# Forgetting attention with its heads in pairs: score products alternate between the two row halves, value products carry high and low parts in one operand

## The chip, the core and the metric

The kernel runs on one core of a Trainium2 chip. The metric is the device time of one execution in microseconds (us). The core has a matrix engine (TensorE, PE in the profile, with its weight loads as PEld), a vector engine (VectorE, DVE), an activation engine (ScalarE, ACT), a general engine (GpSimd, POOL) and queues that start transfers (SyncE, SP). Products go from PE into eight banks of the accumulation memory (PSUM); DVE and ACT read them out of there.

## What is computed

Two transformer blocks of width 1024 on 512 tokens. The change lies in the first block's attention, in the eight "forgetting" heads: causal softmax attention whose logits get a bias from cumulated forget gates.

```python
def forgetting_attention(q, k, v, log_f):
    b, s, h, d = q.shape          # 1, 512, 8, 64
    c = jnp.cumsum(log_f, axis=1)
    ...
        sc = jnp.einsum('bqhd,bshd->bhqs', qi, k).astype(jnp.float32) * scale
        bias = jnp.transpose(ci, (0, 2, 1))[..., None] - c_keys[:, :, None, :]
        causal = kpos[None, :] <= qpos[:, None]
        sc = jnp.where(causal[None, None], sc + bias, -jnp.inf)
        p = jax.nn.softmax(sc, axis=-1).astype(v.dtype)
        return jnp.einsum('bhqs,bshd->bqhd', p, v)
```

The rest of the first block is a projection of the normalised tokens (w_in), eight sliding-window heads, an output projection with residual, and a squared-relu MLP. The second block has its own attention and MLP. All inputs are 32-bit floats.

## The kernel before

Every 32-bit operand is split into a high and a low part, each of a one-pass format, and a product is three passes: high by high, high by low, low by high (`mm3`, lines 151 to 154). `split` (line 146) writes the high part with ACT (line 147) and the low part with DVE (line 148). Transposes are products with an identity matrix.

`attention_one` is one phase. `project` computes the projection in chunks of 384 columns, token tile by token tile of 128 tokens: chunks 0 and 1 for the sliding-window heads (tiles named `pj`, `ta`, `sa`, `oa`), chunks 2 to 5 for the four pairs of forgetting heads (`project_b`). `gates` makes the operands `bq` and `bk` of the gate bias: DVE copies each head's log gate to 4 of 32 columns (line 548), PE sums them up along the tokens (tile `cps`, line 558).

`attn_b(pair, ...)` handles two heads. The queries of head 0 lie in partitions 0 to 63, those of head 1 in 64 to 127. Its steps are (u, h, tt): half of the tokens u, head h, token tile tt in the half. For query tile t = 2u + tt the step covers n = 128 (t + 1) keys:

- `scores`: five products into one bank of the ring `s` (two banks, 5 and 6): three of 64 rows (queries by keys, high and low), the causal mask as a product of 128 rows (line 679), the gate bias as a product of 128 rows (line 680) with an operand `bqi` that keeps only this head's rows. Then DVE takes the row maximum (line 683), ACT the exponential with its sum (line 685), DVE the reciprocal (line 686), and DVE or, for the last tile of head 1, ACT scales the row (line 194 or 192). A probability tile has the tag `p`, of which there are three.
- `turn`: t + 1 transposes of the probabilities (tile `tb`, line 703), split into `pbh` and `pbl`.
- `values`: for each key tile three products with 64 stationary columns (line 577): V high by P high, V high by P low, V low by P high. They add up in the one bank of the ring `o` (bank 2). After head 1, `mixed` splits both heads' sums from that bank into `mixT`, the operand of the output projection.

The loop keeps `turn` two steps behind `scores` (LA = 2), and `interleave` spreads the next pair's projection between the steps. The order in which the instructions stand on the engines is made when the program is built: a scheduler in the building layer reorders all of them by its own model of time. Each engine then works off its list in order. For the last pair there is no projection left; what stands between its steps are products of the output projection (tiles `o`, named `o10_0` and so on, in the same ring positions as the projection's banks, and `o10_2`, which needs bank 2).

## Time and profile before

| | |
|---|---|
| device time, 3 runs | 1271.56, 1274.99, 1276.72 us; median 1274.99 |
| profiled execution, first to last instruction (its own total is not listed apart) | 1270.8 us |
| PE busy | 1227.1 us (97%) |
| DVE, ACT, POOL busy | 750.8, 539.2, 257.5 us |
| forgetting heads, first score product to first product of `o10_2` | 122.0 to 238.0 us of the span |
| PE idle in that stretch | 0.90 + 0.20 + 1.87 us |

An engine's busy time counts an instruction from its start to its modelled end. Matmuls overlap: the end of one lies behind the start of the next. How long PE is held by one is therefore read as the distance from its start to the start of the next, not from its duration.

### The profile page before, as it was taken

The numbers are of one execution on the slowest core, as the hardware profiler recorded it, in microseconds if no ns is written. First come the engines' busy times: TensorE is split into PE (matmuls) and PEld (weight loads), VectorE is DVE, ScalarE is ACT, GpSimd is POOL, SyncE is SP. The second block draws the span as 40 slices with busy tenths as digits, with TensorE's granted clock in tenths as the row PEclk, the third lists the DMA queues.
The fourth block names the chain that finished last, engine by engine and source line by source line (L and its number), as shares of the span: only waits on it lengthen the run. The fifth ranks groups of instructions, "written<-read, shape, count | busy, mean of one in ns | idle before, by whom it ended". The sixth has DMA issues, their size and how long they took to land. (4 is left out here: it accounts for less than half of the span.)

```text
span 1270.8 us, 16908 instructions
## 1 busy us (share of the span) xinstructions
PE 1227.1 (97%) x6388; PEld 1027.8 (81%) x6388; DVE 750.8 (59%) x1320; ACT 539.2 (42%) x1032; POOL 257.5 (20%) x328
## 2 busy tenths in 40 slices
...
GB/s 163 64 73 68 26 63 67 133 186 148 198 239 257 234 100 116 63 131 122 67 176 129 51 67 74 64 59 178 82 117 83 100 100 67 130 69 67 149 50 84
DMA packets 147290, 140.22 MB, mean 110 GB/s; under 512 B 14025, under 2 KB 115160, under 8 KB 147208
## 3 DMA queue, kind: packets, MB, share of 16 engines
...
q14 instruction: 32, 0.26, 0.1%
...
## 5 line engine op out<-in xcount | busy, mean ns | idle before, releaser
L898 DVE SCALAR_TENSOR_TENSOR macc<-mod,silu_c,macc 128x1024 f32<-128x1024 f32 x56 | 76.7, 1379 | 13.8 <-DMA mod<-in_w_mod_dram 13.7
L1245 POOL TENSOR_SCALAR ss<-ss 128x1 f32<-128x1 f32 x4 | 1.8, 442 | 328.5 <-ACT sk L1243 328.5
L1280 DVE TENSOR_TENSOR y<-m2d,y 128x512 f32<-128x512 f32 x24 | 16.6, 691 | 60.4 <-PE m2d L154 60.3
L975 DVE SCALAR_TENSOR_TENSOR xa<-m1d,r,xa 128x512 f32<-128x512 f32 x32 | 23.8, 745 | 37.2 <-PE m1d L154 37.2
L147 ACT ACTIVATE m2hid<-m2sq 128x512 fp32r<-128x512 f32 x32 | 20.2, 631 | 38.9 <-DVE m2sq L844 38.9
L147 ACT ACTIVATE m1hid<-m1sq 128x512 fp32r<-128x512 f32 x32 | 20.0, 629 | 38.1 <-DVE m1sq L844 38.1
...
L148 DVE TENSOR_TENSOR m2hid<-m2sq,m2hid 128x512 fp32r<-128x512 f32 x32 | 22.1, 691 | 19.0 <-ACT m2hid L147 18.9
L148 DVE TENSOR_TENSOR npl<-t,nph 128x512 fp32r<-128x512 f32 x32 | 21.7, 681 | 16.4 <-ACT nph L147 16.3
L181 POOL TENSOR_SCALAR w<-w,g_attn 128x384 f32<-128x384 f32 x20 | 26.1, 1314 | 11.2 <-DMA w<-in_w_in_dram 6.6
L148 DVE TENSOR_TENSOR m1hid<-m1sq,m1hid 128x512 fp32r<-128x512 f32 x32 | 21.9, 686 | 9.1 <-ACT m1hid L147 9.1
L194 POOL TENSOR_SCALAR p<-p,d 128x512 f32<-128x512 f32 x8 | 14.0, 1752 | 56.6 <-DVE d L1116 26.3
L683 DVE TENSOR_REDUCE mb<-sb 128x1 f32<-128x128 f32 (+3 forms) x32 | 15.6, 486 | 16.7 <-PE sb L680 16.6
L1115 ACT ACTIVATE p<-s,m 128x512 f32<-128x512 f32 x32 | 22.0, 688 | 6.2 <-DVE m L1113 6.2
L685 ACT ACTIVATE pb<-sb,mb 128x128 f32<-128x128 f32 (+3 forms) x32 | 16.8, 525 | 16.4 <-DVE mb L683 16.1
L843 ACT ACTIVATE m1re<-m1up 128x512 f32<-128x512 f32 x32 | 18.6, 582 | 9.0 <-PE m1up L154 8.7
L1069 POOL TENSOR_TENSOR tb<-G,nam 128x256 f32<-128x256 f32 x24 | 17.7, 765 | 22.6 <-DVE m L1109 12.5
L147 ACT ACTIVATE nph<-t 128x512 fp32r<-128x512 f32 x32 | 19.0, 595 | 7.4 <-PE t L1126 7.2
L844 DVE SCALAR_TENSOR_TENSOR m1sq<-m1up,m1re 128x512 f32<-128x512 f32 x32 | 21.8, 681 | 0.1
L844 DVE SCALAR_TENSOR_TENSOR m2sq<-m2up,m2re 128x512 f32<-128x512 f32 x32 | 21.8, 682 | 0.0
L1126 PE MATMUL t<-ident,p 128*128 128x128 f32 x128 | 18.4, 276 | 1.9 <-DVE npl L148 1.9
L147 ACT ACTIVATE pbh<-tb 128x128 fp32r<-128x128 f32 (+3 forms) x32 | 13.8, 434 | 14.9 <-PE tb L703 14.7
...
## 6 DMA issues: line engine op xcount, KB each, us to landing
...
```

The lines of the kernel that those rows point to most:

```text
L147: self.nc.scalar.activation(out=hi, in_=src, func=AF.Copy)
L148: (eng or self.nc.vector).tensor_tensor(out=lo, in0=src, in1=hi.bitcast(F32), op=ALU.subtract)
L181: eng.tensor_scalar(out=rv[:, i], in0=rv[:, i], scalar1=g, scalar2=None, op0=ALU.mult)
L685: ac(out=pr[:, 0:n], in_=s[:, 0:n], func=AF.Exp, bias=m[:, 0:1], accum_out=den[:, 0:1])
L843: ac(out=r, in_=acc, func=AF.Relu)
L844: nc.vector.scalar_tensor_tensor(out=s, in0=acc, scalar=0.0, in1=r, op0=ALU.max, op1=ALU.mult)
L898: nc.vector.scalar_tensor_tensor(out=accs[s], in0=rw, scalar=sc[:, s, k:k + 1], in1=accs[s], op0=ALU.mult, op1=ALU.add)
L975: nc.vector.scalar_tensor_tensor(out=x[t][:, cols], in0=acc, scalar=r2[:, t:t + 1], in1=x[t][:, cols], op0=ALU.mult, op1=ALU.add)
L1069: nc.gpsimd.tensor_tensor(out=tb[:, h, y], in0=G[:, h, ::-1, o:o + 32][:, :, ::-1], in1=nam[:, y, :].unsqueeze(1).to_broadcast([P, 8, 32]) ...
L1115: ac(out=pr, in_=s, func=AF.Exp, bias=m[:, 2:3], accum_out=den[:, 0:1])
L1126: nc.tensor.transpose(out=tps[:, j * P:(j + 1) * P], in_=pr[:, j * P:(j + 1) * P], identity=self.ident)
L1280: nc.vector.tensor_tensor(out=y[t][:, cols], in0=acc, in1=y[t][:, cols], op=ALU.add)
```

## The change

One step now holds both heads of a pair. Into the two banks of the ring `s`, one per head, go first the eight products of 64 rows, head 0 and head 1 in turn, in an order that is tied down instruction by instruction (`issue_after`). The gate bias is among them: `gates` puts the log gates of all heads into columns 64 to 95 as well, so `bqi` (one tile per pair, not two) has head 0's rows in the lower half and head 1's in the upper. The two causal masks of 128 rows come last. Then come the maximum, exponential, reciprocal and scaling of head 0 and of head 1. The transposes are one step behind (LAB = 1).

The values' high and low parts lie side by side in one tile `vb`, head by head, so that one product has 128 stationary columns, (V high | V low), and each key tile takes two products: by P high and by P low. The bank then holds the high sums in partitions 0 to 63 and the low ones in 64 to 127. After head 1, ACT copies the lower sums of both heads (64 partitions by 512) into a tile of the tag `p`, DVE adds the upper ones to it, and `mixed` splits from that tile.

```diff
-    used = r < 32
+    used = r % 64 < 32
...
-    for h in range(8):
-        c[:, C_PSEL + h] = r // 4 == h
+    for pair in range(4):
+        c[:, C_PSEL + pair] = np.where(r < 64, r // 4 == 2 * pair, r // 4 - 16 == 2 * pair + 1)
...
-            v = v_tiles(f"vb{i}")
+            v = tp.tile([P, NT, 2, 2, 64], F32R, tag="vb", name=f"vb{i}", bufs=2)
...
-                self.split(v[0][:, t, :], v[1][:, t, :], s[:, 256:384])
+                self.split(v[:, t, :, 0], v[:, t, :, 1], s[:, 256:384].rearrange("p (h d) -> p h d", h=2))
...
-                nc.vector.tensor_copy(out=lfx[:, t, 0:32].rearrange("p (h r) -> p h r", r=4),
-                                      in_=zf[:, t, :].unsqueeze(2).to_broadcast([P, 8, 4]))
+                for o in (0, 64):
+                    nc.vector.tensor_copy(out=lfx[:, t, o:o + 32].rearrange("p (h r) -> p h r", r=4),
+                                          in_=zf[:, t, :].unsqueeze(2).to_broadcast([P, 8, 4]))
...
-            vh, vl = v
-            bqi = []
-            for h in range(2):
-                b = tp.tile([P, SEQ], F32R, tag="bqi", name=f"bqi{pair}{h}", bufs=2)
-                nc.vector.tensor_scalar(out=b, in0=bq.bitcast(F32), scalar1=psel[:, 2 * pair + h:2 * pair + h + 1],
-                                        scalar2=None, op0=ALU.mult)
-                bqi.append(b)
-
-            def scores(u, h, tt):
+            bqi = tp.tile([P, SEQ], F32R, tag="bqi", name=f"bqi{pair}", bufs=2)
+            nc.vector.tensor_scalar(out=bqi, in0=bq.bitcast(F32), scalar1=psel[:, pair:pair + 1], scalar2=None, op0=ALU.mult)
+            def scores(u, tt):
                 t = 2 * u + tt
                 n = (t + 1) * P
                 qs = slice(t * P, (t + 1) * P)
-                s = self.ps("s", f"sb{pair}_{t}{h}")
-                rows = slice(64 * h, 64 * h + 64)
-                self.mm3(s[:, 0:n], q[0][rows, qs], q[1][rows, qs], k[0][rows, 0:n], k[1][rows, 0:n], True, False)
-                mm(out=s[:, t * P:n], lhsT=identr, rhs=causal, start=False, stop=False)
-                mm(out=s[:, 0:n], lhsT=bqi[h][:, qs], rhs=bk[:, 0:n], start=False, stop=True)
-                m = self.small("m", f"mb{pair}_{t}{h}")
-                den = self.small("den", f"db{pair}_{t}{h}")
-                nc.vector.tensor_reduce(out=m[:, 0:1], in_=s[:, 0:n], axis=AX.X, op=ALU.max, negate=True)
-                pr = prs[u, h, tt] = tp.tile([P, SEQ], F32, tag="p", name=f"pb{pair}_{t}{h}", bufs=3)
-                ac(out=pr[:, 0:n], in_=s[:, 0:n], func=AF.Exp, bias=m[:, 0:1], accum_out=den[:, 0:1])
-                nc.vector.reciprocal(out=den[:, 0:1], in_=den[:, 0:1])
-                self.scaled(pr[:, 0:n], den[:, 0:1], TURNB[h * 2 + tt])
+                s = [self.ps("s", f"sb{pair}_{t}{h}") for h in range(2)]
+                rows = [slice(64 * h, 64 * h + 64) for h in range(2)]
+                last = None
+                def put(**kw):
+                    nonlocal last
+                    with self.tc.issue_after(last.ins) if last else nullcontext():
+                        last = mm(**kw)
+                for x, (l, r) in enumerate(((q[0], k[0]), (q[0], k[1]), (q[1], k[0]), (bqi, bk))):
+                    for h in range(2):
+                        put(out=s[h][:, 0:n], lhsT=l[rows[h], qs], rhs=r[rows[h], 0:n], start=x == 0, stop=False)
+                for h in range(2):
+                    put(out=s[h][:, t * P:n], lhsT=identr, rhs=causal, start=False, stop=True)
+                for h in range(2):
+                    m = self.small("m", f"mb{pair}_{t}{h}")
+                    den = self.small("den", f"db{pair}_{t}{h}")
+                    nc.vector.tensor_reduce(out=m[:, 0:1], in_=s[h][:, 0:n], axis=AX.X, op=ALU.max, negate=True)
+                    pr = prs[u, h, tt] = tp.tile([P, SEQ], F32, tag="p", name=f"pb{pair}_{t}{h}", bufs=3)
+                    ac(out=pr[:, 0:n], in_=s[h][:, 0:n], func=AF.Exp, bias=m[:, 0:1], accum_out=den[:, 0:1])
+                    nc.vector.reciprocal(out=den[:, 0:1], in_=den[:, 0:1])
+                    self.scaled(pr[:, 0:n], den[:, 0:1], TURNB[h * 2 + tt])
...
-            def values(u, h):
-                if h == 0:
-                    os_[u] = self.ps("o", f"ob{pair}{u}")
-                o = os_[u]
+            def values(o, u, h):
                 pth, ptl = pths.pop((u, h))
                 nj = 2 * u + 2
-                terms = []
+                seq = []
                 for j in range(nj):
                     q0 = P if j == nj - 1 else 0
                     c = slice(h * 256 + q0, h * 256 + 256)
-                    terms.append((c, vh[:, j, :], vl[:, j, :], pth[:, j, q0:256], ptl[:, j, q0:256]))
-                weighted(o, slice(64 * h, 64 * h + 64), terms)
+                    l = v[:, j, h].rearrange("p x d -> p (x d)")
+                    seq += [(c, l, pth[:, j, q0:256]), (c, l, ptl[:, j, q0:256])]
+                seq.append(seq.pop(1))
+                for x, (c, l, r) in enumerate(seq):
+                    mm(out=o[:, c], lhsT=l, rhs=r, start=(x == 0), stop=(x == len(seq) - 1))
                 if h == 1:
-                    mixed(o, mixT[1], pair, u)
-
-            units = [(u, h, tt) for u in range(2) for h in range(2) for tt in range(2)]
-            for x in range(len(units) + LA + 1):
+                    low = tp.tile([P, SEQ], F32, tag="p", name=f"ob{pair}{u}", bufs=3)
+                    ac(out=low[0:64], in_=o[64:128], func=AF.Copy)
+                    nc.vector.tensor_tensor(out=low[0:64], in0=o[0:64], in1=low[0:64], op=ALU.add)
+                    mixed(low, mixT[1], pair, u)
+            units = [(u, tt) for u in range(2) for tt in range(2)]
+            for x in range(len(units) + LAB + 1):
                 if x < len(units):
                     scores(*units[x])
-                    yield CB * 0.45
-                y = x - LA
+                    yield CB * 0.7
+                y = x - LAB
                 if 0 <= y < len(units):
-                    turn(*units[y])
-                    yield CB * 0.27
+                    u, tt = units[y]
+                    for h in range(2):
+                        turn(u, h, tt)
+                        yield CB * 0.27
                 y -= 1
                 if y >= 0 and y % 2 == 1:
-                    u, h, _ = units[y]
-                    values(u, h)
-                    yield CB * 0.8
+                    u, _ = units[y]
+                    os_[u] = self.ps("o", f"ob{pair}{u}")
+                    for h in range(2):
+                        values(os_[u], u, h)
+                        yield CB * 0.55
```

On PE a score step of the second pair stands like this before (head 0, query tiles 0 and 1, five products each):

```order
L152 MATMUL sb1_00_2009<-kb1h_1604,qb1h_1602 128x128
L153 MATMUL sb1_00_2009<-kb1l_1605,qb1h_1602 128x128
L154 MATMUL sb1_00_2009<-kb1h_1604,qb1l_1603 128x128
L679 MATMUL sb1_00_2009<-causal_136,identr_137 128x128
L680 MATMUL sb1_00_2009<-bk_153,bqi10_2005 128x128
L152 MATMUL sb1_10_2035<-kb1h_1604,qb1h_1602 128x256
L153 MATMUL sb1_10_2035<-kb1l_1605,qb1h_1602 128x256
L154 MATMUL sb1_10_2035<-kb1h_1604,qb1l_1603 128x256
L679 MATMUL sb1_10_2035<-causal_136,identr_137 128x128
L680 MATMUL sb1_10_2035<-bk_153,bqi10_2005 128x256
```

After the change, the step of query tile 1, both heads (the last digit of `sb1_10` and `sb1_11` is the head):

```order
L682 MATMUL sb1_10_2039<-kb1h_1618,qb1h_1616 128x256
L682 MATMUL sb1_11_2040<-kb1h_1618,qb1h_1616 128x256
L682 MATMUL sb1_10_2039<-kb1l_1619,qb1h_1616 128x256
L682 MATMUL sb1_11_2040<-kb1l_1619,qb1h_1616 128x256
L682 MATMUL sb1_10_2039<-kb1h_1618,qb1l_1617 128x256
L682 MATMUL sb1_11_2040<-kb1h_1618,qb1l_1617 128x256
L682 MATMUL sb1_10_2039<-bk_153,bqi1_1999 128x256
L682 MATMUL sb1_11_2040<-bk_153,bqi1_1999 128x256
L682 MATMUL sb1_10_2039<-causal_136,identr_137 128x128
L682 MATMUL sb1_11_2040<-causal_136,identr_137 128x128
```

The 64-row products of the two heads alternate, the bias is one of them, and the masks stand at the end.

On PE in the last pair (pair 3) before, round the score step of head 0, query tile 1 (`sb3_10`; `o10_1` is a tile of the output projection):

```order
L154 MATMUL o10_1_3091<-o1w01h_3040,mixT0_499 128x512
L152 MATMUL o10_1_3091<-o1w02h_3046,mixT1_1584 128x512
L153 MATMUL o10_1_3091<-o1w02l_3047,mixT1_1584 128x512
L152 MATMUL sb3_10_2822<-kb3h_2444,qb3h_2442 128x256
L153 MATMUL sb3_10_2822<-kb3l_2445,qb3h_2442 128x256
L154 MATMUL sb3_10_2822<-kb3h_2444,qb3l_2443 128x256
L679 MATMUL sb3_10_2822<-causal_136,identr_137 128x128
L680 MATMUL sb3_10_2822<-bk_153,bqi30_2805 128x256
L154 MATMUL o10_1_3091<-o1w02h_3046,mixT1_1584 128x512
L152 MATMUL o10_1_3091<-o1w02h_3046,mixT1_1584 128x512
L153 MATMUL o10_1_3091<-o1w02l_3047,mixT1_1584 128x512
L154 MATMUL o10_1_3091<-o1w02h_3046,mixT1_1584 128x512
```

After the change the same place, from the masks of query tile 1 (`sb3_10`, `sb3_11`) through the transposes of query tile 0 (`tb3_00`, `tb3_01`) to the bias of query tile 2:

```order
L682 MATMUL sb3_10_2809<-causal_136,identr_137 128x128
L682 MATMUL sb3_11_2810<-causal_136,identr_137 128x128
L711 MATMUL tb3_00_2837<-ident_78,pb3_00_2798 128x128
L711 MATMUL tb3_01_2841<-ident_78,pb3_01_2805 128x128
L682 MATMUL sb3_20_2845<-kb3h_2440,qb3h_2438 128x384
L682 MATMUL sb3_21_2846<-kb3h_2440,qb3h_2438 128x384
L682 MATMUL sb3_20_2845<-kb3l_2441,qb3h_2438 128x384
L682 MATMUL sb3_21_2846<-kb3l_2441,qb3h_2438 128x384
L682 MATMUL sb3_20_2845<-kb3h_2440,qb3l_2439 128x384
L682 MATMUL sb3_21_2846<-kb3h_2440,qb3l_2439 128x384
L682 MATMUL sb3_20_2845<-bk_153,bqi3_2781 128x384
L682 MATMUL sb3_21_2846<-bk_153,bqi3_2781 128x384
```

No product of the output projection is left between the score steps of the last pair there; those of `o10_0` and `o10_1` that need no result of it stand ahead, in the pair before.

On ACT, at the passage from pair 2 to pair 3, after the change (`ob21_2693` is the copy of the lower sums, written by line 731; `pb3_00` the exponential of the last pair's first scores):

```order
L149 ACTIVATE pbh210_2589<-tb2_30_2633 128x4x128
L149 ACTIVATE pbh211_2600<-tb2_31_2643 128x4x128
L731 ACTIVATE ob21_2693<-ob21_2653 64x512
L693 ACTIVATE pb3_00_2798,db3_00_2796<-sb3_00_2783,mb3_00_2795 128x128
L693 ACTIVATE pb3_01_2805,db3_01_2803<-sb3_01_2784,mb3_01_2802 128x128
```

The exponential of the last pair's first scores stands behind the copy of pair 2's value sums, which has no counterpart in the list of before.

On DVE in `gates`, before:

```order
L543 SCALAR_TENSOR_TENSOR zf_142<-zf_142,az_500 128x32
L548 COPY lfx_505<-zf_142 128x32 x4
L465 SCALAR_TENSOR_TENSOR qa_143<-ta00_0_308,misc_124,qa_143 64x256
L554 CAST trir_516<-traw_514 128x896
L605 ISA sa0_0_536,ma0_0_537<-sa0_0_536,alibi_490,misc_124 128x128
```

After the change:

```order
L545 SCALAR_TENSOR_TENSOR zf_142<-zf_142,az_500 128x32
L551 COPY lfx_505<-zf_142 128x32 x7
L467 SCALAR_TENSOR_TENSOR qa_143<-ta00_0_308,misc_124,qa_143 64x256
L551 COPY lfx_505<-zf_142 128x32
L608 ISA sa0_0_540,ma0_0_541<-sa0_0_540,alibi_490,misc_124 128x128
L608 ISA ma0_0_541 128x1
L557 CAST trir_520<-traw_518 128x896
L608 ISA sa0_0_540,ma0_0_541<-sa0_0_540,alibi_490,misc_124 128x128
```

There are eight copies in place of four ahead of the cast to `trir`, the operand that PE's first product of `cps` waits for, and the custom instruction on `sa0_0` (line 605 before, 608 after) stands ahead of that cast, too, where it stood behind it.

## Rows read from the trace of the kernel before

**Rows 1.** The page: busy time, share of the span, instructions of each engine.
```profile
PE 1227.1 (97%) x6388; PEld 1027.8 (81%) x6388; DVE 750.8 (59%) x1320; ACT 539.2 (42%) x1032; POOL 257.5 (20%) x328
```

**Rows 2.** Stretches: us, busy us of PE PEld DVE ACT POOL; PEclk, DMA, GB/s.
```profile
177.50:210.00 32.50, 32.50 (x192) 27.28 (x191) 21.87 (x53) 18.81 (x45) 9.63 (x14) 1.00 0.18 65
210.00:238.00 28.00, 25.04 (x158) 19.36 (x156) 16.91 (x45) 15.16 (x40) 4.02 (x6) 1.00 0.13 42
238.00:241.50 3.50, 3.49 (x9) 2.72 (x10) 1.18 (x2) 0.00 (x0) 2.51 (x2) 0.53 1.04 376
```

**Rows 3.** Timeline, PE, one score step (start, duration, then line and operands).
```profile
135.39 0.33 PE L152 MATMUL pj<-w_3h,xnT 128*128 128x384 f32 x1
135.65 0.44 PE L152 MATMUL sb<-kb0h,qb0h 64*128 64x384 f32 x1
135.93 0.33 PE L153 MATMUL sb<-kb0l,qb0h 64*128 64x384 f32 x1
136.11 0.33 PE L154 MATMUL sb<-kb0h,qb0l 64*128 64x384 f32 x1
136.37 0.33 PE L679 MATMUL sb<-causal,identr 128*128 128x128 f32 x1
136.53 0.39 PE L680 MATMUL sb<-bk,bqi 128*128 128x384 f32 x1
136.76 0.34 PE L153 MATMUL pj<-w_3l,xnT 128*128 128x384 f32 x1
```

**Rows 4.** Timeline, PE, second block's attention: 64-row products of two heads.
```profile
692.83 0.28 PE L154 MATMUL s<-kT,qT 64*128 64x256 f32 x1
692.83 0.28 PE L153 MATMUL s<-kc,qT 64*128 64x256 f32 x1
692.95 0.28 PE L152 MATMUL s<-kc,qT 64*128 64x256 f32 x1
```

**Rows 5.** Timeline, PE: value products of pair 0, transposes of pair 3.
```profile
158.38 0.28 PE L577 MATMUL ob<-pbh,vb0l 128*64 128x256 f32 x1
158.50 0.22 PE L577 MATMUL ob<-pbh,vb0h 128*64 128x128 f32 x1
158.56 0.22 PE L577 MATMUL ob<-pbl,vb0h 128*64 128x128 f32 x1
...
229.35 0.60 PE L703 MATMUL tb<-ident,pb 128*128 128x128 f32 x4
```

**Rows 6.** Groups, 122 to 238 us: busy us, mean ns | idle before.
```profile
L683 DVE TENSOR_REDUCE mb<-sb 128x1 f32<-128x512 f32 x8 | 5.5, 689 | 5.1 <-PE sb L680 5.1
L685 ACT ACTIVATE pb<-sb,mb 128x512 f32<-128x512 f32 x8 | 5.5, 688 | 7.2 <-DVE mb L683 7.0
L685 ACT ACTIVATION_READ_ACCUMULATOR pb<-sb,mb 128x1 f32 x32 | 6.3, 197 | 0.0
L192 ACT ACTIVATE pb<-pb,db 128x512 f32<-128x512 f32 x4 | 2.9, 722 | 0.3 <-DVE db L686 0.2
L147 ACT ACTIVATE pbh<-tb 128x512 fp32r<-128x512 f32 x8 | 4.7, 594 | 7.5 <-PE tb L703 7.4
L148 DVE TENSOR_TENSOR pbl<-tb,pbh 128x512 fp32r<-128x512 f32 x8 | 5.5, 686 | 2.1 <-ACT pbh L147 2.1
L147 ACT ACTIVATE mixT<-ob 64x256 fp32r<-64x256 f32 x16 | 6.0, 375 | 6.8 <-PE ob L577 6.2 <-DVE mixT L148 0.5
```

**Rows 7.** Timeline, PE: its two long waits at the end of pair 3.
```profile
230.85 0.52 PE L703 MATMUL tb<-ident,pb 128*128 128x128 f32 x3 [0.90 <-DVE db L686]
...
238.01 0.58 PE L152 MATMUL o<-o1w00h,mixT 128*128 128x512 f32 x1 [1.87 <-DVE mixT L148]
```

**Rows 8.** Timeline, gates: DVE's copies and cast, PE's wait for them.
```profile
41.80 1.37 DVE L548 COPY lfx<-zf 128x32 f32<-128x32 f32 x4
...
44.26 0.35 DVE L605 CUSTOM_DVE_ANT_0 sa<-sa,alibi,misc 128x128 f32<-128x128 f32 x1
...
44.49 0.77 PE L558 MATMUL cps<-trir,lfh 128*128 128x512 f32 x1 [2.71 <-DVE trir L554]
```

3 lines of the change are left out of this document (2 added, 1 removed).

## Prediction

> **What bounds the kernel now.** First the page: PE is busy for 97% of the span, no other engine for more than 59% [rows 1]. The stage that the change touches runs from 122.0 to 238.0 us, and two stretches of it are to be told apart [rows 2]. In 177.5 to 210, a stretch of the earlier pairs, PE is busy for 32.50 of 32.50 us; DVE is at 21.87 us (67%), ACT at 18.81 us (58%). PE time saved there is time saved, for as long as DVE and ACT keep up. In 210 to 238, the last pair, PE is busy for 25.04 of 28.00 us. Its idle 2.96 us hold two waits with a price of their own, 0.90 us for a reciprocal and 1.87 us for `mixT` [rows 7]; both lie at the end, when no output projection that could be done ahead is left. What comes after the first product of `o10_2` at 238.01 has the same order before and after the change but for a few neighbours, so I count what moves that point and carry it to the end. All terms are differences against the profiled span of 1270.8 us; the median of the runs, 1274.99 us, is 0.3% above it, and the sum is added to the median.
>
> **Score products.** One step of 384 keys shows where PE's time goes [rows 3]. From one `pj` product to the next are 1.37 us, with 0.18 for `pj` itself, 3 x 0.18 for the score products, 0.06 for the mask and 0.18 for the bias. That makes 0.95; the other 0.42 are switching: 0.085 from 128 to 64 rows, 0.10 behind the first product, 0.085 back to 128 rows, 0.10 behind the mask, 0.055 behind the bias. A product holds PE for 0.18 at 384 columns, for 0.12 at 256 [rows 4], by scale for 0.235 at 512. At 128 columns behind a weight load of 128 columns it is an estimated 0.11: four such transposes take 0.60, one alone some 0.25 of that, a third of the rest each [rows 5].
>
> Before: 32 steps x (0.42 + 0.06) plus rounding make 15.7; seven further entries to 64 rows, where the order breaks a step up with other products, at 0.37 make 2.6; eight heads x 4 products x (0.11 + 0.12 + 0.18 + 0.235) make 20.5. Together 38.8 us.
>
> After: does the second head's product run beside the first's? The second block does this already: a product of one head starts at 692.83, that of the other, in the other half of the rows, at 692.83 too, and the next at 692.95 [rows 4]. So the streams fall to half, 10.2, with 0.8 for first products that run alone. Sixteen steps cost 0.085 + 0.10 + 0.085 of switching and 0.27 for the two masks, 0.54 each, 8.6 together; ten further entries (by the order, 26 stand for 16 steps) at 0.38 make 3.8. Sum 23.5, **15.3 us less**. If the halves didn't run side by side the streams would stay at 20.5, and 10.2 of this would be gone.
>
> **Value products.** A product of 256 columns holds PE for 0.12 (158.38 to 158.50), one of 128 columns for 0.06, both with 64 stationary columns [rows 5]. A head takes 3 x 0.12 + 3 x 0.06 = 0.54 in the first half of the tokens and 9 x 0.12 + 3 x 0.06 = 1.25 in the second. After: 2 x 0.12 + 2 x 0.11 = 0.46 and 6 x 0.12 + 2 x 0.11 = 0.93, where the 0.11 stands for 128 moving columns behind 128 stationary ones. Eight heads save 8 x (0.08 + 0.32) = **3.2 us**. PE's work falls by 18.5 us.
>
> **The last pair.** Before, the steps of one head lie two apart, and products of `o10_1` stand between them. After, none is left there, and a step takes both banks of the ring `s`: the next step's first product waits until both exponentials have read them. For 512 keys these are 0.69 (maximum), 0.69 and 0.20 (exponential and its sum), then 0.72 (scaling) before a transpose can start, and 0.59 and 0.69 for `pbh` and `pbl` behind it [rows 6]. I laid the order of all three engines out by hand with such durations, from the last masks of pair 2 to the first product of `o10_2`. It came to 29.75 us with PE idle for 12.8: 1.55 for the banks at the first step of pair 3; 1.0 for products that wait for pair 2's `mixT` (0.38 an ACT piece [rows 6]), now behind the copy and the addition; 1.3 at query tile 1, whose exponentials stand behind that copy on ACT; 1.7 and 1.2 at the banks of query tiles 2 and 3; 1.8 and 1.3 at the transposes of query tile 3; 1.3 for `mixT` in between; 1.65 at the end, with copy and addition ahead of `mixed`. Against 3.0 before this is **+9.8 us**. The low bound, +3, is a last pair that waits for two such ends in place of one; the high one, +14, has every bank wait last 0.7 longer, which is one more instruction of DVE or ACT in front.
>
> **Pairs 0 to 2.** DVE loses nothing of its work but the four scalings for `bqi`, and gets eight additions; with PE's time shorter by about a sixth, its 67% [rows 2] become some 80%. The projection's products (0.18 each [rows 3]) still stand between the steps. I take **+1.5 us** of small waits where only five or six of them do, from 0 to 13 (rival B).
>
> **Gates.** Four copies take 1.37 us on DVE ahead of the cast for which PE waits 2.71 us at `cps` [rows 8]. Four more are 1.37 again, and the custom instruction that is now ahead of the cast holds DVE for 0.26 (44.26 to 44.52). Nothing covers this: PE has no other work in front of `cps`. **+1.6 us**, from 0 (should DVE come to it earlier) to 2.2 (the low part `lfh` is written later too).
>
> **PE's clock.** Behind the 1.87 us wait the granted clock was 0.53 for the 3.5 us from 238.0 on, 1.00 before [rows 2]: about the lower of the two levels, 1.2 against 2.4 GHz, and 1.65 us lost in it. The last pair would idle a dozen times, for 1 to 2 us each. I take two more stretches like this one, rounded to **+3 us**, from 0 to 4.
>
> **The sum:** -18.5 + 9.8 + 1.5 + 1.6 + 3.0 = -2.6 us, so 1275.0 - 2.6 = **1272.4 us**. About 0.5%, or 6.4 us, is what the measurement can tell from no change.
>
> **Rival A, faster: the last pair barely waits.** My chain took each wait at its full length with the engines' lists in strict order. If exponentials and maxima overlap better than that, the wait is +3 in place of +9.8 and the clock stays up: -18.5 + 3 + 1.5 + 1.6 = -12.4, or 1262.6 us. For it: the last pair before had 25.04 busy of 28.00 us though its steps wait for the same kinds of results [rows 2]. Against it: those steps had products of the output projection between them.
>
> **Rival B, slower: both banks bind everywhere.** With two banks for two heads, no step's scores can begin before both maxima and exponentials of the step before are done. At 512 keys, two maxima and two exponentials in a chain over two engines are 0.69 + 2 x (0.69 + 0.20) = 2.5 us [rows 6]; a third of that uncovered, in the eleven steps of pairs 0 to 2 that follow another, is 1.2 us more each at PE, some +13, and the sum becomes +10: 1285 us. It decides from about 0.85 us of wait per step on, where the sum passes +6.4. Against it: the projection's products between two steps, usually eight or more, cover 1.4 us and the transposes a further part. Beside this stands a rule of the Trainium skill, TensorEngine Tiling (Array Packing), section PSUM Bottleneck: tiling makes TensorE faster but not the reading of PSUM, which can then become the bottleneck, so ScalarE and VectorE should both read. The trace of before agrees only in that both do read it here, and DVE is the next engine after PE; whether it becomes the bound no row can show.
>
> **Rival C: the halves don't overlap.** The change then doesn't do what it says; 10.2 us come back and the time is 1282.6 us. For it: the pairs in that row have 256 columns, here they have up to 512, and the bias has other operands. Against it: [rows 4] shows just such pairs.
>
> **How the numbers follow.** Forecast, within 0.5%: 0.52. Rival A 0.32, rival B 0.09, rival C 0.07; B and C both end over 6.4 us slower. So faster 0.32, same 0.52, slower 0.16. The range should leave out 2 in 10: its low end, 1261, takes in rival A and little beyond, its high end, 1282, all of the forecast's bounds in the last pair (+14 in place of +9.8, clock +4: 1277.6) with some waits of pairs 0 to 2, and ends short of B and C.
>
> **What would show each step.** The score products of both heads start at the same times in pairs, and `sb` and `ob` products together hold PE some 18 us less. `cps` starts near 46.1. From the last pair's first scores to `o10_2` PE idles some 13 us, in waits of 1 to 2 us, for DVE and ACT; and the clock is below 1.00 in more than one stretch there. The first product of `o10_2` stands between 232 and 236 us on the span. If instead PE waits between the steps of pairs 0 to 2, with DVE or ACT as the releaser, it is rival B; if the last pair shows 6 us of idle or less, rival A. The prediction is wrong if some engine off this path, the weights' loads or POOL's splits, turns out late once PE comes to them earlier: POOL was at 30% in 177.5 to 210 (9.63 us [rows 2]).

## The result, and the profile after

The changed kernel takes 1294.29 us (median of 4 runs, 1291.0 to 1295.05) against 1273.28 us for the kernel before, timed beside it (4 runs, 1269.57 to 1276.72). The ratio is 1.0162, with a 95% interval of 1.0136 to 1.0189: slower by about 21 us. The forecast was 1272.4, its range 1261 to 1282. The result lies outside the range, on the side of rival B. The profiled execution has a span of 1293.3 us, 22.5 more than before.

The page of the changed kernel, to be set beside [rows 1]: 48 products fewer, yet PE is busy for longer, and for a smaller share.

```profile
PE 1230.9 (95%) x6340; PEld 1032.9 (80%) x6340; DVE 761.0 (59%) x1328; ACT 541.8 (42%) x1040; POOL 254.3 (20%) x328
```

Stretches of the changed kernel, columns as in [rows 2]: up to the first score product; from there to the last pair's first score; the last pair up to `o10_2`; the rest. The second fence has the same four cuts in the kernel before.

```profile
0.00:133.73 133.73, 111.89 (x655) 105.06 (x655) 97.29 (x281) 81.36 (x214) 80.26 (x102) 0.91 0.31 79
133.73:222.67 88.94, 83.10 (x518) 71.56 (x517) 62.98 (x155) 54.02 (x145) 41.67 (x52) 0.96 0.23 68
222.67:256.22 33.55, 27.11 (x124) 21.61 (x124) 18.33 (x48) 16.65 (x44) 1.71 (x3) 0.69 0.19 60
256.22:1293.30 1037.08, 1008.81 (x5044) 834.65 (x5044) 582.39 (x846) 389.79 (x640) 130.68 (x172) 0.99 0.38 117
```

```profile
0.00:121.99 121.99, 106.13 (x655) 99.73 (x655) 92.27 (x279) 83.02 (x221) 81.38 (x102) 0.97 0.34 87
121.99:210.37 88.38, 88.38 (x538) 75.06 (x538) 62.49 (x155) 52.52 (x137) 42.80 (x52) 1.00 0.22 69
210.37:238.01 27.64, 24.67 (x154) 19.17 (x154) 16.92 (x45) 14.84 (x40) 4.02 (x6) 1.00 0.13 43
238.01:1270.80 1032.79, 1007.94 (x5044) 833.87 (x5044) 579.13 (x843) 388.85 (x638) 129.28 (x169) 0.99 0.38 118
```

Two things stand out. The first score product is 11.7 us late, before any product that the change was made for. And the last pair has 30 products fewer than before, but PE is busy in it for 27.11 us in place of 24.67, because the granted clock is 0.69: most of it ran at the lower of the two levels, 1.2 against 2.4 GHz.

To keep such effects apart I cut each profiled execution into pieces of 2 us and add up three shares: **idle** (length less PE's busy time), **low clock** (busy time times one less the granted clock) and **work**, what is left: PE's busy time as it would be at full clock (an estimate: where the clock is low it comes out some 2 us too small, see below the table of runs). "Stage" runs from the first score product to the first product of `o10_2`.

| kernel | first score at | stage | idle | low clock | work | rest | span |
|---|---|---|---|---|---|---|---|
| before | 121.99 | 116.0 | 3.0 | 0 | 113.1 | 1032.8 | 1270.8 |
| after | 133.73 | 122.5 | 12.2 | 12.2 | 98.0 | 1037.1 | 1293.3 |

So of the 22.5 us, +11.7 lie ahead of the stage (idle +6.0, low clock +6.7, work -1.0), +6.5 in it (work -15.1, idle +9.2, low clock +12.2), and +4.3 behind it, where 3.2 are one wait of PE at `m1d`, a tile of the first block's MLP, for DVE's `xa` (5.11 us against 1.87).

The waits of PE in the stage of the changed kernel (who waits, for whom, total, times, longest), the main ones:

```profile
PE sb L682 <- ACT pb L693: 5.4, 7, 1.3
PE o L154 <- ACT pjs L409: 2.3, 1, 2.3
PE tb L711 <- DVE db L694: 1.7, 1, 1.7
PE o L154 <- DVE ob L732: 1.4, 1, 1.4
```

Before, the list was 1.9, 0.9 and 0.2 us (the two longer ones in [rows 7]). The first line is what rival B named: scores that wait until the exponentials have left the two banks; 2.9 of its 5.4 us lie up to the last pair's first score, the rest behind it. In the timeline of PE, the first scores of three steps of the last pair (start, duration, operands, wait):

```profile
222.67 0.32 PE L682 MATMUL sb<-kb3h,qb3h 64*128 64x128 f32 x1 [1.30 <-ACT pb L693]
...
233.19 0.38 PE L682 MATMUL sb<-kb3h,qb3h 64*128 64x256 f32 x1 [1.17 <-ACT pb L693]
...
235.96 0.44 PE L682 MATMUL sb<-kb3h,qb3h 64*128 64x384 f32 x1 [1.06 <-ACT pb L693]
```

The halves of the rows do overlap, as [rows 4] let expect. A paired step with 512 keys, in the timeline of PE (its first product stands alone, ahead of value products):

```profile
182.81 0.49 PE L682 MATMUL sb<-kb1h,qb1h 64*128 64x512 f32 x1
...
183.73 0.49 PE L682 MATMUL sb<-kb1h,qb1h 64*128 64x512 f32 x1
183.73 0.72 PE L682 MATMUL sb<-kb1l,qb1h 64*128 64x512 f32 x2
184.07 0.61 PE L682 MATMUL sb<-kb1h,qb1l 64*128 64x512 f32 x2
184.29 0.62 PE L682 MATMUL sb<-bk,bqi 64*128 64x512 f32 x2
184.84 0.44 PE L682 MATMUL sb<-causal,identr 128*128 128x128 f32 x2
185.12 0.41 PE L711 MATMUL tb<-ident,pb 128*128 128x128 f32 x2
```

Two products start at 183.73, and the last seven of the step's eight take 1.11 us (183.73 to 184.84), with the passage to 128 rows in it. At 0.235 each, one behind the other, the seven alone would be 1.65. The Trainium skill says so too (TensorE: Matmul & The Clock Gate, Part 3: Packing small matmuls): products in different row groups run concurrently.

### The profile page after: what moved, and what is told of

Its sections match the earlier page's. It is cut to its first block, busy times and chain, and to the rows that moved or that the text cites. A ratio compares the mean times of both kernels' runs of the same rounds, so it can differ in the third digit from the quotient of the medians.

```text
span 1293.3 us, 16848 instructions
## 1 busy us (share of the span) xinstructions
PE 1230.9 (95%) x6340; PEld 1032.9 (80%) x6340; DVE 761.0 (59%) x1328; ACT 541.8 (42%) x1040; POOL 254.3 (20%) x328
## 5 line engine op out<-in xcount | busy, mean ns | idle before, releaser
L914 DVE SCALAR_TENSOR_TENSOR macc<-mod,silu_c,macc 128x1024 f32<-128x1024 f32 x56 | 76.3, 1378 | 12.1 <-DMA mod<-in_w_mod_dram 11.9
L991 DVE SCALAR_TENSOR_TENSOR xa<-m1d,r,xa 128x512 f32<-128x512 f32 x32 | 23.5, 746 | 41.8 <-PE m1d L156 41.8
L150 DVE TENSOR_TENSOR m2hid<-m2sq,m2hid 128x512 fp32r<-128x512 f32 x32 | 22.1, 691 | 19.0 <-ACT m2hid L149 18.9
L154 PE MATMUL pj<-w_0h,xnT 128*128 128x384 f32 (+1 forms) x48 | 19.0, 395 | 5.5 <-ACT pjs L409 4.1
L149 ACT ACTIVATE mh<-macc 128x1024 fp32r<-128x1024 f32 x8 | 8.5, 1059 | 28.9 <-DVE macc L914 12.7
L1142 PE MATMUL t<-ident,p 128*128 128x128 f32 x128 | 18.9, 280 | 1.7 <-DVE npl L150 1.7
```

The costliest lines, as they stand in the source:

```text
L149: self.nc.scalar.activation(out=hi, in_=src, func=AF.Copy)
L150: (eng or self.nc.vector).tensor_tensor(out=lo, in0=src, in1=hi.bitcast(F32), op=ALU.subtract)
L154: mm(out=out, lhsT=lh, rhs=rh, start=start, stop=False)
L914: nc.vector.scalar_tensor_tensor(out=accs[s], in0=rw, scalar=sc[:, s, k:k + 1], in1=accs[s], op0=ALU.mult, op1=ALU.add)
L991: nc.vector.scalar_tensor_tensor(out=x[t][:, cols], in0=acc, scalar=r2[:, t:t + 1], in1=x[t][:, cols], op0=ALU.mult, op1=ALU.add)
L1142: nc.tensor.transpose(out=tps[:, j * P:(j + 1) * P], in_=pr[:, j * P:(j + 1) * P], identity=self.ident)
```

## Experiments

Ratios are to the kernel before, timed beside each kernel, with 95% intervals. A kernel is called by the part of its label ahead of the underscore. Kernels g2, n2, b4, w2, p1, p2, p4, p5, c1, c2, f1 and h2 share one edit (`g2_wide`), so that the late start doesn't blur what they show of the stage. The filler products of w2, f1, h1 and h2 write into a bank that nobody reads.

| kernel | first score at | stage | idle | low clock | work | rest | ratio (95%) |
|---|---|---|---|---|---|---|---|
| g1_copies | 133.35 | 117.2 | 4.2 | 0.1 | 112.9 | 1034.5 | 1.0104 (1.0066 to 1.0143) |
| g6_late | 133.38 | 117.2 | 4.2 | 0 | 113.0 | 1033.0 | 1.0099 (1.0082 to 1.0116) |
| g2_wide | 123.71 | 123.0 | 13.1 | 10.1 | 99.8 | 1035.3 | 1.0126 (1.0092 to 1.016) |
| m0_before | 130.55 | 116.4 | 4.2 | 0 | 112.3 | 1030.6 | 1.0044 (1.0022 to 1.0066) |
| m1_after | 126.17 | 122.4 | 12.1 | 10.2 | 100.1 | 1036.0 | 1.0147 (1.0115 to 1.0178) |
| v1_values | 121.45 | 113.2 | 3.2 | 0 | 109.9 | 1037.1 | 1.0033 (1.0016 to 1.005) |
| n2_inturn | 124.67 | 125.8 | 10.4 | 12.2 | 103.2 | 1033.2 | 1.0124 (1.009 to 1.0157) |
| p2_singles | 124.92 | 115.0 | 3.6 | 0 | 111.5 | 1034.4 | 1.0013 (0.9996 to 1.003) |
| p4_single23 | 124.34 | 113.9 | 7.1 | 1.7 | 105.2 | 1035.5 | 1.0027 (1.0016 to 1.0039) |
| p5_single13 | 125.41 | 114.2 | 5.1 | 3.4 | 105.7 | 1028.5 | 0.9979 (0.996 to 0.9998) |
| p1_single3 | 124.64 | 113.3 | 5.6 | 5.0 | 102.7 | 1028.3 | 0.9982 (0.9964 to 1.0000) |
| b4_banks | 125.56 | 122.0 | 10.7 | 12.8 | 98.5 | 1033.2 | 1.0069 (1.0045 to 1.0092) |
| c1_dve | 124.45 | 123.6 | 12.2 | 11.9 | 99.5 | 1035.5 | 1.0097 (1.008 to 1.0114) |
| c2_dve13 | 122.33 | 111.8 | 5.7 | 1.3 | 104.7 | 1030.5 | 0.9989 (0.9977 to 1.0002) |
| w2_last | 124.22 | 120.2 | 8.6 | 1.5 | 110.2 | 1037.1 | 1.0094 (1.0063 to 1.0125) |
| f1_fill | 125.43 | 115.1 | 7.8 | 2.7 | 104.6 | 1027.9 | 0.999 (0.9971 to 1.0008) |
| h1_before | 120.88 | 116.0 | 1.3 | 0 | 114.7 | 1030.7 | 1.0001 (0.9987 to 1.0016) |
| h2_p5 | 123.46 | 113.9 | 3.5 | 3.4 | 107.0 | 1028.5 | 0.998 (0.9966 to 0.9994) |

Of w2's work 8.5 us are its filler (36 products at 0.235). That leaves 101.7, 1.9 more than g2 has at a lower clock with the same products, and 3.7 more than the changed kernel: low clock as added up here holds some time that a full clock would not give back, and differences of work between kernels at different clocks are good to 2 us or so. The times in single traces scatter, too: h1 and the kernel before, h2 and p5 have the same order of instructions but for the filler, and their first scores lie 1.11 and 1.95 us apart.

### Why the first score is late: the gates

**g1_copies** is the kernel before with nothing but the eight copies.

```diff
-                nc.vector.tensor_copy(out=lfx[:, t, 0:32].rearrange("p (h r) -> p h r", r=4),
-                                      in_=zf[:, t, :].unsqueeze(2).to_broadcast([P, 8, 4]))
+                for o in (0, 64):
+                    nc.vector.tensor_copy(out=lfx[:, t, o:o + 32].rearrange("p (h r) -> p h r", r=4),
+                                          in_=zf[:, t, :].unsqueeze(2).to_broadcast([P, 8, 4]))
```

> The kernel before with one edit: the log gates are copied to columns 64 to 95 as well (eight copies, as in the change; the extra rows are multiplied by zero later). Theory C (the gates' waits take the clock down, and that is most of the early loss): the first forgetting score comes 8 to 12 us later than before (130 to 134 us on the span against 122.0), with the granted clock at 0.5 behind the wait at cps, and the time rises by 7 to 12 us. Theory S (the copies cost only themselves, the early loss of the changed kernel has another origin): rise of 1 to 3 us, first score at 123 to 125.

The first score stands at 133.35, as late as after the whole change, and the kernel is 1% slower, by 13 us. **g2_wide** is the changed kernel with one copy per token tile that writes both groups of columns.

```diff
-                for o in (0, 64):
-                    nc.vector.tensor_copy(out=lfx[:, t, o:o + 32].rearrange("p (h r) -> p h r", r=4),
-                                          in_=zf[:, t, :].unsqueeze(2).to_broadcast([P, 8, 4]))
+                nc.vector.tensor_copy(out=lfx[:, t, :].rearrange("p (o c) -> p o c", o=2)[:, :, 0:32].rearrange("p o (h r) -> p o h r", r=4),
+                                      in_=zf[:, t, :].unsqueeze(2).unsqueeze(1).to_broadcast([P, 2, 8, 4]))
```

> The changed kernel with the eight copies made as four, each of which writes both groups of columns (64 elements in place of 32). Theory C: the early stage stands in the order of before, the first score comes at 122 to 124 us, and 7 to 12 us of the 21 come back (1282 to 1287 us). Theory S: 1 to 3 us come back (1291 to 1293 us).

The start is back at 123.71, some 10 us earlier. (The other 2 us lie ahead of the gates, where the order is that of before: from 24 to 28 us the granted clock is 0.64 after the change, and 0.52, 0.66 and 0.59 in g1, g6 and g2, but 1.00 in before, v1 and h1, though PE has waited as long there in v1 and h1. I don't put them down to the change.) By ratios g2 is only 0.36% below the change, with intervals that overlap.

The copies' own time isn't the cause: seven of the eight take 1.15 us after the change, where the four took 1.37 before [rows 8]. What differs is DVE's list behind them. DVE's low part `lfh`, in the kernel before and then after the change (with the copies, and the reduce `a03ss` now ahead of it):

```profile
44.52 0.69 DVE L148 TENSOR_TENSOR lfh<-lfx,lfh 128x512 fp32r<-128x512 f32 x1
```

```profile
44.36 1.15 DVE L551 COPY lfx<-zf 128x32 f32<-128x32 f32 x7
...
47.91 0.49 DVE L452 TENSOR_REDUCE a03ss<-a03sq 128x5 f32<-128x320 f32 x1
48.31 2.04 DVE L150 TENSOR_TENSOR lfh<-lfx,lfh 128x512 fp32r<-128x512 f32 x1
```

It now comes behind several other instructions, and beside an instruction of POOL; then PE waits twice at `cps` (POOL's row, and PE's two, of the changed kernel):

```profile
47.99 1.82 POOL L150 TENSOR_TENSOR w_3l<-w,w_3h 128x768 fp32r<-128x768 f32 x1 [3.03 <-ACT w_3h L149]
```

```profile
47.23 0.79 PE L561 MATMUL cps<-trir,lfh 128*128 128x512 f32 x1 [3.52 <-ACT lfh L149]
...
50.41 0.80 PE L561 MATMUL cps<-trir,lfh 128*128 128x512 f32 x1 [1.10 <-DVE lfh L150]
```

**g6_late** tests the order without added work: the kernel before, with its four copies, no work added, and that one subtraction tied behind the reduce `a03ss`.

```diff
-            self.split(lfh[:, 0], lfh[:, 1], lfx)
+            nc.scalar.activation(out=lfh[:, 0], in_=lfx, func=AF.Copy)
+            with tc.issue_after(self.red.ins):
+                nc.vector.tensor_tensor(out=lfh[:, 1], in0=lfx, in1=lfh[:, 0].bitcast(F32), op=ALU.subtract)
```

> The kernel before, four copies as before, with one thing tied: the subtraction that writes the low part of the gates (lfh, on DVE) comes after the reduction a03ss instead of ahead of a qa operand, the place that it has in the changed kernel. Theory O (what the eight copies cost is the order of DVE's list: the low part falls beside POOL's w_3l, where it took 2.04 us in place of 0.69, PE waits for it, the clock falls, and DVE, busy for over 90% from 50 to 120 us, does not make it up): the first forgetting score comes 4 to 10 us later than before, time 1276 to 1282 us. Theory D (the copies themselves): within 2 us of before.

The first score is at 133.38 and the ratio 1.0099: the same 1% as with eight copies, though nothing was added. `lfh` takes 1.75 us there, and the planner sets what follows the gates in another order too: on PE, seven of the eight products of `cps` now stand behind three transposes that they stood ahead of, as they do after the change. So the order is the cause; which part of it (`lfh` late, `lfh` beside POOL, or the transposes) isn't told apart. A stretch of 10 us just behind the gates bears on why the loss isn't made up (after, then before):

```profile
50.00:60.00 10.00, 9.59 (x41) 8.92 (x42) 7.06 (x18) 4.62 (x15) 6.05 (x6) 0.71 0.34 80
```

```profile
50.00:60.00 10.00, 10.00 (x60) 9.93 (x60) 9.81 (x27) 6.11 (x19) 7.63 (x10) 0.98 0.17 44
```

Before, DVE is busy for 9.81 of these 10 us, and for 8.8 to 9.8 of every ten up to 120. After, with PE at 0.71 of its clock, DVE does only 7.06 in them. That what DVE loses there it can't catch up is argued from these shares.

**m0_before, m1_after** move the call of `gates` behind the first projection chunk, in the kernel before and in the changed one (`gates()` one line lower, behind the loop's first `interleave`).

> The kernel before with one edit: gates() stands behind the first two pairs of sliding-window heads instead of ahead of them, so that the cumulated sums (cps) find their operands ready. Theory C: the wait of 2.71 us at cps and the 3.4 us of low clock behind it go, 4 to 6 us faster than before, with the first forgetting score at 116 to 118 us on the span. Rival S (DVE, at 90% or more in this stretch, only shifts its delay to another wait): within 2 us of before.

> The changed kernel with the same edit as m0_before, still with eight copies. Theory C: all that the gates cost goes, the 11.7 us by which the first score is late and the 4 to 6 us that the gates cost before, too: 12 to 17 us faster than the changed kernel, 1277 to 1282 us. Rival S: no more than 9 us, what g2_wide gave.

The idea falls: m0 is 0.4% slower than before, its first score at 130.55. PE waits elsewhere, for ACT (2.02 us at 46.5, 2.04 at 93.9). m1 starts at 126.17 and stays at 1.0147.

### Do the halves and the values bring what was counted?

**v1_values** is the kernel before with the values' part of the change alone (`vb`, two products a key tile, the copy and the addition).

```diff
-                    terms.append((c, vh[:, j, :], vl[:, j, :], pth[:, j, q0:256], ptl[:, j, q0:256]))
-                weighted(o, slice(64 * h, 64 * h + 64), terms)
+                    l = v[:, j, h].rearrange("p x d -> p (x d)")
+                    seq += [(c, l, pth[:, j, q0:256]), (c, l, ptl[:, j, q0:256])]
...
+                    ac(out=low[0:64], in_=o[64:128], func=AF.Copy)
+                    nc.vector.tensor_tensor(out=low[0:64], in0=o[0:64], in1=low[0:64], op=ALU.add)
```

> The kernel before with the value products alone changed: V's high and low parts as one operand, copy of the lower sums and addition; scores as before, head by head. The sum of the prediction: 3.2 us less PE work, some 1.3 us more at the end of the last pair (copy and addition ahead of mixT), so 1 to 3 us faster than before if the clock stays as it is. If the copy on ACT and the addition on DVE make waits of their own in pairs 0 to 2: 0 to 4 us slower.

Work falls from 113.1 to 109.9, the 3.2 us of the forecast, and the stage by 2.8. Still the kernel is 0.3% slower: the rest is 4.3 us longer, with the longer wait at `m1d` (4.6 us).

**n2_inturn** is g2_wide with head 0's four products first, then head 1's.

```diff
-                for x, (l, r) in enumerate(((q[0], k[0]), (q[0], k[1]), (q[1], k[0]), (bqi, bk))):
-                    for h in range(2):
+                for h in range(2):
+                    for x, (l, r) in enumerate(((q[0], k[0]), (q[0], k[1]), (q[1], k[0]), (bqi, bk))):
```

> As g2_wide, but in each step the four 64-row products of head 0 are issued before the four of head 1, so that no product has one of the other half beside it. Theory P (the halves run side by side): PE's score work rises by 8 to 10 us; some of it falls into waits of the last pair, so 5 to 10 us slower than g2_wide. Rival (the halves don't overlap, or the stage is bound by DVE and ACT): within 2 us of g2_wide.

Work rises by 3.4 only. In the timeline of PE, a step of n2, the second head begins before the first is through:

```profile
164.28 0.28 PE L681 MATMUL sb<-kb1l,qb1h 64*128 64x256 f32 x1
164.40 0.28 PE L681 MATMUL sb<-kb1h,qb1l 64*128 64x256 f32 x1
164.41 0.38 PE L681 MATMUL sb<-kb1h,qb1h 64*128 64x256 f32 x1
164.52 0.27 PE L681 MATMUL sb<-bk,bqi 64*128 64x256 f32 x1
164.63 0.28 PE L681 MATMUL sb<-kb1l,qb1h 64*128 64x256 f32 x1
```

Where both banks are free in time, all four start in pairs, though they are issued head by head:

```profile
172.32 0.45 PE L681 MATMUL sb<-kb1h,qb1h 64*128 64x384 f32 x2
172.60 0.34 PE L681 MATMUL sb<-kb1l,qb1h 64*128 64x384 f32 x2
```

So n2 can't stand for "no overlap", as I had meant it to. What pairing brings is read from the next runs instead.

### Which pairs to pair

In p1, p2, p4 and p5 the pairs named in `SINGLE` go head by head as before (one bank a step, `turn` two steps behind, the copy in a tile of its own), with the change's operands. p1 is `SINGLE = (3,)`, p5 (1, 3), p4 (2, 3), p2 all four.

```diff
-                for h in range(2):
+                for h in hs:
...
+            if pair in SINGLE:
+                units = [(u, h, tt) for u in range(2) for h in range(2) for tt in range(2)]
+                for x in range(len(units) + LA + 1):
+                    if x < len(units):
+                        u, h, tt = units[x]
+                        scores(u, tt, (h,))
...
```

> As g2_wide, but the last pair goes head by head as before the change (a step takes one bank of the ring s, transposes two steps behind), with the bias of 64 rows and the value products of the change; pairs 0 to 2 stay paired. If the waits of the last pair come from both banks being taken by one step: idle time behind the first score of pair 3 falls from 5.5 to 3 or less, the low clock there from 8.5 to 4 or less, and the time is 4 to 8 us below g2_wide. If they come from the missing cover (no output projection left between the steps): within 2 us of g2_wide.

> As p1_single3, but all four pairs go head by head: no two products of different halves beside each other, 64-row bias and value products as in the change. If pairing is worth the 8 to 10 us of PE's time that half the streams are: PE's full-speed work between first score and o10_2 rises from 102.7 us (p1_single3) to 108 to 110, the waits and the low clock of pairs 0 to 2 (2.2 and 5.0 us) go, so 0 to 3 us slower than p1_single3. If pairing is worth little: 3 to 6 us faster than p1_single3.

> As p1_single3, with pair 2 head by head, too. Pair 2 runs while the projection for pair 3 ends, so it loses its cover in its second half. If double use of the banks costs there as in pair 3: 1 to 4 us faster than p1_single3. If pair 2 has cover enough: 0 to 3 us slower (PE work of one pair's overlap, some 1 to 2 us).

> As p1_single3, with pair 1 head by head, too; pairs 0 and 2 stay paired. Pair 1 is where p1_single3 idles 2.2 us and loses 5.0 us to the low clock. If those come from pair 1's paired steps: the low clock in the stage falls to 2 us or less, PE's work rises by 2 to 3 us, the stage takes 109 to 112 us. If they come from pair 0's end: still some 5 us of low clock, and the stage takes 114 to 117 us.

From p2 to p4, p1 and g2 (none, two, three and four pairs paired) work falls by 6.3, 2.5 and 2.9, or 11.7 for four pairs: nearly 3 us a pair (9.8 in all if g2's work is read from w2). This is two heads in one step as a whole, the overlap and fewer changes between 64 and 128 rows. But idle and low clock together are 3.6, 8.8, 10.6 and 23.2: pairing the last pair saves 2.9 and costs 12.6. The last pair of g2 and of p1, from the first score to `o10_2`:

```profile
216.02:246.71 30.69, 25.18 (x124) 19.40 (x124) 17.95 (x48) 16.40 (x44) 1.70 (x3) 0.72 0.19 61
```

```profile
212.94:237.94 25.00, 21.56 (x125) 16.42 (x124) 16.54 (x45) 15.74 (x43) 4.14 (x6) 0.99 0.29 94
```

Of the 9.7 us that p1's stage is shorter than g2's, 5.7 lie behind the last pair's first score. Another 4.2 lie between the first scores of pairs 1 and 2 (32.07 us in g2, 27.85 in p1), though these are paired in both: the planner's order differs, and in g2 PE waits 2.08 us there for the copy of a projection, 0.24 in p1. Both kernels have 12 products of the output projection in the last pair, six of them between its first steps, where the kernel before has 22, so their lack alone isn't what slows g2. In p1 the copy of the lower sums has a tile of its own, too, and no run changes that alone; in g2's last pair no long wait of ACT ends with the release of a tile `p`, its longest end with value products (3.71 us) and maxima (3.45).

What p5 was to decide it leaves open: its low clock of 3.4 lies between its two expectations, its stage of 114.2 at the edge of the second.

p1 takes 1267.67 us and p5 1267.03, with 1270.45 and 1271.38 for the kernel before beside them: 0.2% under it, each at the edge of what can be told apart. By ratios to the kernel before they lie 1.4% below g2_wide; of the 15.8 us between the spans of g2 and p1, 7.0 lie behind the stage.

### What in the paired last pair is slow

**b4_banks** gives it four banks in place of two (banks 0 and 1, which the projection no longer needs, join the ring).

```diff
+            if i == 3:
+                self.rings["s"] = [5, 6, 0, 1]
```

> As g2_wide (all four pairs paired), but for the last pair the ring of score banks has four banks in place of two (the projection's two are free by then; the output projection's first tiles get theirs later). If the last pair waits because each step takes both banks and the next can't start (rival B of the prediction, in the last pair): PE's waits before score products of pair 3 go, the low clock from the first score of pair 3 to o10_2 falls from 8.5 us to 4 or less, and the time falls by 4 to 10 us against g2_wide (1275 to 1281). If the waits come from the chain through DVE and ACT or from the missing cover, they move to the transposes: within 2 us of g2_wide.

The stage shortens by 1.0 us only, with 23.5 of idle and low clock as before (23.2). The waits move: 2.3 us are left at the banks (4.9 in g2), and 2.8 stand at the value products for DVE's `pbl` (1.4 in g2). By ratios b4 lies 0.57% below g2, some 7 us, with intervals that touch, but only 1.3 us of it are in the spans; and the planner draws steps of pair 3 forward into pair 2 (its first score is at 208.07), so more than the banks has changed.

**c1_dve** and **c2_dve13** give the copy of the lower sums to DVE, in g2 and in p5.

```diff
-                    ac(out=low[0:64], in_=o[64:128], func=AF.Copy)
+                    nc.vector.tensor_copy(out=low[0:64], in_=o[64:128])
```

> As g2_wide, with the copy of the lower value sums on DVE in place of ACT. In g2_wide that copy stands on ACT ahead of the exponentials of pair 3's first scores, which end their maxima at 218.7 us and start at 223.4. If that place in ACT's list makes the end of the stage late: the exponentials start within 1 us of their maxima, the stretch from pair 2's last masks to o10_2 falls from 32.3 to 27 to 30 us, and the time by 3 to 6 us (1279 to 1282). If the steps' own chains pace it: within 2 us of g2_wide.

> As p5_single13, with the copy on DVE in place of ACT. If the copy's place on ACT costs there too: 1 to 3 us faster than p5_single13 (1264 to 1266 us); else the addition on DVE makes it 0 to 2 us slower.

ACT in g2, then in c1, at the passage to the last pair: the exponentials no longer stand behind a copy that waits 2.23 us.

```profile
222.81 0.59 ACT L730 ACTIVATE ob<-ob 64x512 f32<-64x512 f32 x1 [2.23 <-PE ob L727]
223.43 0.37 ACT L692 ACTIVATE pb<-sb,mb 128x128 f32<-128x128 f32 x1
```

```profile
221.43 0.36 ACT L692 ACTIVATE pb<-sb,mb 128x128 f32<-128x128 f32 x1
```

Yet the last pair takes 30.78 us with it, 30.69 without. (By ratios c1 is 0.3% below g2, with intervals that overlap.) Neither the banks nor the copy are shown to be the cause alone. What remains, argued from these runs and from p1 and not shown: both heads' maxima, exponentials, scalings and splits come in one burst, and PE has no product of the other head to do meanwhile. c2 has the shortest stage of all (111.8), but its time is level with the kernel before.

### What the low clock costs

**w2_last** is g2_wide with 36 filler products in the waits of the last two pairs, each group tied to a place.

```diff
+        WARM = {(2, 1): 8, (2, 3): 5, (3, 0): 4, (3, 1): 4, (3, 2): 3, (3, 3): 6, (3, 4): 6}
...
+            for _ in range(k_):
+                with tc.issue_after(last.ins):
+                    last = mm(out=wt, lhsT=identr, rhs=bk, start=True, stop=True)
```

> As g2_wide, with products that nobody needs (128 by 512, into a bank of the transposes) put into PE's waits: 8 behind the masks of pair 2's query tile 1, 5 behind its query tile 3, 4, 4, 3 and 6 behind those of pair 3, 6 behind its last value products. They take away no wait; they keep PE at work in it. Theory C (the low clock behind the waits is what the end of the stage costs): of the some 10 us that g2_wide loses at granted clock 0.5 between 200 and 247 us on the span most come back, less 1 to 3 us for the added work: 5 to 9 us faster than g2_wide, 1276 to 1280 us. Rival E (DVE and ACT are the limit, the clock does not matter): no faster, up to 4 us slower.

The last pair of w2, to be set beside g2's row above:

```profile
216.19:244.47 28.28, 24.70 (x148) 18.86 (x147) 18.83 (x48) 17.02 (x46) 1.18 (x2) 1.00 0.10 30
```

The clock is at 1.00 throughout, and the pair takes 2.4 us less. Low clock as added up above was 7.1 us of g2's last pair ((1 - 0.72) x 25.18): a third of it comes back, net of the filler's own time; that the rest is paced by DVE and ACT is the reading that remains, with the planner's order changed by the filler, too. On the whole time w2 lies 0.3% below g2, with intervals that overlap: that doesn't tell the two theories apart.

**f1_fill** puts seven such products behind a value product of pair 0 in p1.

```diff
+                    if (pair, u, h, x) == (0, 1, 0, 1):
+                        wt = self.ps("t", "warm")
+                        for _ in range(7):
+                            with tc.issue_after(end.ins):
+                                end = mm(out=wt, lhsT=identr, rhs=bk, start=True, stop=True)
```

> As p1_single3, with seven products that nobody needs (128 by 512, 0.235 us each, 1.65 us together, into a bank of the transposes) behind the second value product of pair 0's second half, where PE waits 1.61 us for pbl at 160.6 and has granted clock 0.5 for some 10 us behind it (5.0 us lost). The wait is not made shorter; PE only stays at work in it. Theory C (the clock falls because of the wait, and that is what costs): the low clock between 160 and 174 us goes, and the stage from first score to o10_2 falls from 113.3 to 108 to 110 us. Rival E (that stretch is paced by DVE and ACT, a full clock would only wait): 113 to 115 us.

Inconclusive: the ties made the planner put two weight splits ahead of exponentials on ACT, and a new wait took the place of the old (ACT, then PE, of f1):

```profile
164.72 0.84 ACT L150 ACTIVATE w_3h<-w 128x768 fp32r<-128x768 f32 x1 [2.49 <-POOL w L184]
```

```profile
168.87 0.69 PE L684 MATMUL sb<-kb1h,qb1h 64*128 64x384 f32 x1 [4.45 <-ACT pb L695]
```

**h1_before** and **h2_p5** put the seven products behind pair 3's last value product, in the kernel before and in p5; no other instruction moves.

```diff
+                if (pair, u, h) == (3, 1, 1):
+                    wt = self.ps("t", "warm")
+                    for _ in range(7):
+                        with tc.issue_after(end.ins):
+                            end = mm(out=wt, lhsT=identr, rhs=bk, start=True, stop=True)
```

> The kernel before with seven products of 128x512 into an unused bank, whose result nobody reads, tied behind the last value product of pair 3; they lie in the wait of 1.87 us ahead of o10_2 [rows 7] and move no other instruction on any engine. Theory (a low clock behind a wait is time that comes back): the granted clock is 1.00 in the 3.5 us behind o10_2's first product, which was 0.53, so some 1.6 us of that stretch return; o10_2's first product starts where it did, within 0.3 us; the total falls by 1 to 2 us, 0.999. Rival (the low clock has no price of its own, because the stretch behind waits for something else): the clock rises but the next stretch is as long as before, ratio 1.000.

> p5_single13 (pairs 0 and 2 paired, pairs 1 and 3 head by head) with the same seven unused products behind the last value product of pair 3, no other instruction moved. Theory: clock 1.00 behind o10_2's first product, 1 to 2 us less than p5_single13, ratio to the kernel before about 0.997. Rival: clock raised or not, the same time as p5_single13, 0.998.

h1's stretch behind the first product of `o10_2`, to be set beside the third line of [rows 2]:

```profile
236.91:240.41 3.50, 3.50 (x15) 2.88 (x16) 1.31 (x3) 0.00 (x0) 3.17 (x5) 1.00 0.90 239
```

Fifteen products in 3.5 us where there were nine. From the first product of `o10_2` to the 25th are 5.65 us, 7.21 before: 1.56 us returned, as the 1.65 of the forecast had it, with the stage unchanged at 116.0. On the whole time this doesn't show: 1.0001, with an interval (0.9987 to 1.0016) at whose very edge 1.6 us lies. In p5 there was nothing to regain: the clock was already up behind its wait of 1.40 us (5.68 us to the 25th product, 5.62 in h2), while p1, behind a wait of the same 1.40, needed 7.06.

## Why the prediction was wrong

**PE's work: right in kind, 3.4 us or more too high.** Forecast -18.5, measured -15.1 in the stage. Value products came out exactly (-3.2 in v1). Read from w2, at full clock and without its filler, the fall is 11.4, so the miss is between 3.4 and 7.1. The score products were the term: 15.3 counted, 10.1 from v1 to g2 (pairing brings 11.7 from p2 to g2, but the change's operands head by head cost 1.6, v1 to p2). Added up from start to next start at the granted clock, score products hold PE for 33.9 us before and 22.5 after (23.7 in w2). With 0.085 on the neighbour for each of 39 and 26 entries to 64 rows these are 37.2 and 24.7, an estimate, where 38.8 and 23.5 were counted: too much before, too little after.

**Gates: the step that failed first.** +1.6 us was forecast; the first score is 11.7 us late. "Four more are 1.37 again" priced the work of the copies; the bound for a later `lfh` was 0.6 us more. The eight copies were 0.5 to 1.0 us longer than the four (44.36 to 46.23, with another instruction between them; the four took 1.37 before, 0.89 in v1 and g6), but in DVE's new order `lfh` begins 3.95 us behind the first copy (2.72 before) and lasts 2.04 us in place of 0.69, and DVE, at some 9 us and more in 10 up to 120 us, did not make up for it. The price is some 10 us at the first score (133.4 in g1 and g6, 123.7 in g2), and 1% of the time when it is alone (g1, g6: +13 us by their ratios). In the full change it is less clear, since g2 removes it and the ratio falls by 0.36% only, though the profiled span is 11.3 us shorter. I had read DVE's share for the stage and not ahead of it, where it is nearly full from 50 us on. For `lfh` beside POOL's `w_3l` the Trainium skill has a rule (SBUF — State Buffer, Who interferes with whom): a VectorE instruction with two SBUF inputs contends with a GpSimd instruction that reads SBUF, and whichever comes second is blocked until the first is done. The rows agree in the main: 2.04 us where POOL's instruction began 0.32 us ahead, and the end 0.54 us behind POOL's own end at 49.81 (0.55 in g1 and g6), a little less than the whole 0.69 that it takes where POOL was idle. No run took POOL's instruction away.

**The last pair: the length of the chain was near, its idle and its clock were not.** The hand-made chain gave 29.75 us from the last masks of pair 2 to `o10_2`. It is 30.08 in w2, whose clock there is 1.00, but 32.29 in g2 and 35.31 after the change, where the clock is 0.72 and 0.69 in the last pair. But its 12.8 us of idle aren't there: from the last pair's first score PE idles 6.4 us after the change (5.5 in g2), 3.5 more than before, with 1.3 ahead of it, where +9.8 was forecast. The waits at the banks, at the transposes of query tile 3 and at the end are there, mostly shorter; the two for `mixT` are not. What I had not laid out is that the products between them run at half speed: 9.7 us of low clock lie in this stretch, which fill the waits and lengthen the chain. That the sum of 29.75 fits w2 so well is in part luck, with filler in its waits.

**Clock: the term that was most under-sized.** "Two more stretches like this one", +3 with an upper bound of 4, stands against 12.2 us in the stage and 6.7 ahead of it. Not all of it is a price: an isolated wait costs what the forecast said (1.56 us in h1), but in the last pair only a third came back in w2.

**Pairs 0 to 2 and rival B.** +1.5 us of small waits was the forecast; idle in that stretch is 5.8 us, low clock 2.5. They take all of the 7.8 us of work saved there (88.94 us after, 88.38 before). Of the idle, 2.9 are at the banks and 2.7 at products that wait for ACT's copy of a projection (`pjs`), which the forecast had not laid out. Rival B had a chance of 0.09 and a price of +13 in pairs 0 to 2, and the time it gave, 1285, is nearer to the measured one than the forecast; but a third of 2.5 us is 0.8 and not 1.2, so by its own words the price was some +9 and the time 1281. Its mechanism, PE held up because the exponentials have not left the banks, is there, 5.4 us in seven waits. But it has 2.9 us in pairs 0 to 2, not 13: against the kernel before, the stage is longer by 0.6 us there and by 5.9 in the last pair. In pairs 0 and 1 idle and low clock grow by 5.2 for 6.3 of work saved (p2 to p4), no gain worth naming; in pair 2 by 1.8 for 2.5. With four banks in the last pair (b4) the stage still loses 23.5 us to idle and low clock. The rule of the Trainium skill that the prediction set beside this rival (TensorEngine Tiling (Array Packing), PSUM Bottleneck) is borne out in part: PE does wait for exponentials to leave PSUM, 3.8 us in the four waits from 222.67 on. But ScalarE and VectorE both read, and neither is full there (16.65 and 18.33 of 33.55 us): it is a chain of results that binds, not the rate of reading.

**Rival A and rival C.** Rival C is out: the halves overlap. The sign set for rival A, 6 us of idle or less in the last pair, is nearly met (6.4, and 5.5 in g2), but not its time: low clock came in place of the idle, which that sign didn't see.

**The sum.** With the terms as measured: work -16.1 (of it -1.0 ahead of the stage), idle +15.2, low clock +18.9, rest +4.3 is +22.3, the 22.5 of the spans but for rounding. Of the 25 us between this and the forecast's -2.6, 18 are idle and low clock (+34.1, where 9.8 + 1.5 + 1.6 + 3.0 = 15.9 were counted), 4 the rest, and 2 PE's work.

**What stays open.** The rest behind `o10_2` has the same products in all kernels and varies between 1027.9 and 1037.1 us; the forecast put no change there. The wait at `m1d` for `xa` is 4 us and more in after, v1, g2, n2, w2, m1, p4, b4 and c1, 3.8 in c2, and under 2 in all others. It is some 3 us of the change's 22.5, and I have no run that tells why.
